# A two-layer hybrid attention trunk on one core: the causal mask of the stick-breaking mixer moved from identity matmuls to VectorE adds in PSUM, and the output stage split in the middle

## The chip, the core and the metric

The kernel runs on one core of a Trainium2 chip. The core has a matmul engine (TensorE, PE in the profile, with its weight loads as PEld), three elementwise engines (VectorE is DVE, ScalarE is ACT, GpSimd is POOL) and a queue engine (SyncE, SP) that here only issues transfers. Each engine runs its own list of instructions in order and waits on semaphores for the others. TensorE writes to PSUM, eight banks of 512 float32 per partition, and VectorE and ScalarE read and write there as well. The metric is the time of one execution on the device in microseconds, as the median of several runs.

## What is computed

Two layers on 512 tokens of width 1024. A layer normalises its input, projects it to some 8,000 columns, runs three causal token mixers (A: sparse attention with a top-k choice of keys; B: a sliding window of 128; C: stick-breaking attention), gates and projects each mixer's output, adds the three and projects the sum back onto the residual stream. A last RMS norm gives the output. Mixer C is the one whose mask is touched:

```python
strict = (key_pos[None, :] < qpos[:, None])[None, None]
z = jnp.einsum('bthd,bshd->bhts', qb, k).astype(jnp.float32) * (dh ** -0.5)
log_beta = jax.nn.log_sigmoid(z)
log_1m = jnp.where(strict, jax.nn.log_sigmoid(-z), 0.0)
after = lax.cumsum(log_1m, axis=3, reverse=True) - log_1m
a = jnp.where(strict, jnp.exp(log_beta + after), 0.0)
return jnp.einsum('bhts,bshd->bthd', a.astype(v.dtype), v)
```

and the output stage is `x + gate * (merged @ w_out)`, after the last layer followed by `y * rsqrt(mean(x*x) + EPS) * g`.

## The kernel before

Everything is kept with features or keys laid out so that TensorE works on 128x128 weights and up to 512 columns. Each float32 product is made of three matmuls in a faster 32-bit type: a matrix is split into a high part (a cast) and a remainder (a subtraction), and high x high, high x low and low x high are summed in PSUM. So for each weight tile that arrives (`wstage`), a cast makes `whi` and a subtraction makes `wlo`. Either may run on several engines.

The order of the work is not written by hand. The program is recorded as a list of instructions, some with alternatives on two or three engines, and a planner (`Recorder`) plays it forward with prices for each operation (`price`), picks at each step an engine and an instruction by priority, takes new priorities from the latest possible starts (`latest`), repeats this five times and keeps the best (`order`). The order it ends with is what each engine runs. GpSimd operations that share a memory port with VectorE get an explicit dependency on the VectorE operation ahead of them. All instructions are emitted from one line (L596 in the profile; pairs of small tiled matmuls from L594), so groups are told apart by their tiles.

A layer's stages: `first_phase` and `v_phase` project the first columns and the values. Then the three mixers run one after another, C first, woven with the projections of what comes later (`uh`, `ul` times `whi`, `wlo` into the banks `ps_z`), with the top-k search of mixer A (`score`, on VectorE) and with the branch projections. Last comes `out_phase`.

Mixer C takes its 8 heads in 4 pairs. For a pair, `c_qk` fills five banks `ps_s` with scores: nine matmuls of `KH` and `klow` against `Q`, and for each of 4 query blocks and 2 heads one matmul of an identity with a mask in bfloat16 (`ident_b`, `cmask_b`), which adds a large negative number on and above the diagonal of the last 128 columns. Seven small matmuls (`low_parts`) add the low parts of the keys; in pairs 1 to 3 the values of the pair before (`t`, `vc`) ride in the same instruction group and are then evacuated by `finish_pair` (`e`, `Y`). Then each bank goes through an absolute value (on ScalarE or VectorE), an exponential, a logarithm, a minimum with a subtraction, a reverse scan (VectorE) and a last exponential; the result `t` is transposed by TensorE (20 transposes with the identity in `small`) for the product with the values. The banks are released by the scans.

`out_phase` makes eight output tiles from the merged branches (`mh`, `ml`, which lie in the buffers `vc`, `va`, `Q`, `KH`). The last two (`tail`) are made in two column parts, so that the norm of the first part can start before the second is done. `update` adds the residual, squares, sums the squares into `m` and scales by the final gain; `rstd` sums over partitions by a matmul with `nones` and takes the logarithm and the exponential; `after` multiplies and, in the last layer, sends the products out. In layer 0 the parts are 256 and 256 columns, in the last layer 320 and 192.

`load_consts` loads the rotary tables and the masks and casts identity and mask to bfloat16.

Of the kernel before, what the change touches and what calls it, by code (L numbers as in the profile page):

```python
# [260 lines left out]
class Recorder:  # L261
# [75 lines left out]
    def price(self, x, engine, op, args, kw):  # L337
# [17 lines left out]
        if engine == "PE":  # L355
# [6 lines left out]
            elif op == "transpose":  # L362
                c, y.mode = 0.1085, "t"
                y.cost, y.lag = c, c + self.PIPE
            else:
                rhs, y.mode = args[2], "m"
                c = 4 * n / 2.4e3 + 0.01 if rhs.dtype == F32 else 0.06 if rhs.dtype == BF16 else (n + 33.5) / 2.4e3
                y.cost, y.lag = c, c + self.PIPE
# [41 lines left out]
    def forward(self):  # L410
# [38 lines left out]
        while len(out) < len(self.list):  # L449
# [51 lines left out]
            if y.mode == "dma":  # L501
                x.end = dma_free = max(at + (2.1 if at < 20.0 else 3.0), dma_free) + y.lag * (1.6 if dma_free < 5.5 else 0.955 if at < 20.0 else 1.0)
                lanes.append(x.end)
# [40 lines left out]
    def latest(self, end, out):  # L544

        late = {x.i: end - x.hold for x in out}
        after, first = {}, {}
# [76 lines left out]
def trunk(ctx, tc, xT, vecs, w_ss, w_gt, w_first, w_t, w_v, w_br, w_o, rope, consts, out):  # L624
# [541 lines left out]
    def c_qk(p):  # L1166
        def fn():
# [3 lines left out]
            for i in (3, 2, 0, 1):  # L1171
# [7 lines left out]
                for e in range(2):  # L1179
                    mm(o[e], q[:, e, ts], kh[:, e, :W], first[e])  # L1180
                for e in range(2):
                    mm(o[e][:, W - 128:], ident_b, cmask_b, False)
                if i == 1:
                    mm(o[1], q[:, 1, ts], kl[:, S:], False)
            low_parts(q, kl, apos, zb, "c", p, LOW_ALL)
            for bk in (0, 3, 1, 4, 2):
                z = zb[bk]
                t = pt[bk] = t512("t", 10)
                u32 = mybir.dt.uint32
# [273 lines left out]
    def out_phase(l):  # L1463
# [34 lines left out]
        def after(cs_):  # L1498
            rstd(cs_)
            if l + 1 < L:  # L1500
                if cs_.start == 0:
                    st["uh"], st["ul"] = [None] * KT, [None] * KT
                for k in (0, 1):
                    times_rstd(st["xn"][k], cs_)
                    make_u(l + 1, k, st["xn"][k], cs_)
                return
            w = cs_.stop - cs_.start
            for d in range(KT):
                if d % 2 == 0 or w > S // 2:
                    o, n = t512("t", 10), 0  # L1510
                v, a = o[:, n:n + w], st["xn"][d][:, cs_]
                n += w
                if d in (2, 4):
                    POOL.tensor_tensor(out=v, in0=a, in1=st["rstd_sb"][:, cs_], op=OP.mult)
                else:
                    DVE.tensor_tensor(out=v, in0=a, in1=st["rstd"][:, cs_], op=OP.mult)
                if w > S // 2:
                    SP.dma_start(out[:, d, cs_], v)
                elif d % 2:
                    SP.dma_start(out[:, d - 1:d + 1, cs_], o[:, :n].rearrange("p (a b) -> p a b", a=2))  # L1520

# [8 lines left out]
        def tail(*ws):  # L1530
            z, xr = [zbank(), zbank()], [load(6), load(7)]
            for cs_ in HALVES if l + 1 < L else (slice(0, 320), slice(320, S)):
                for i in range(2):
                    mms(6 + i, ws[2 * i:2 * i + 2], z[i], cs_)
                    update(6 + i, z[i], xr[i], cs_)
                after(cs_)
            save(6)
            save(7)
            st["x"] = st["xn"]
            if l + 1 < L:  # L1540
                st["xold"] = st["xsave"]
# [77 lines left out]

    sin_t = cos_t = tri0 = band = ident_b = cmask_b = None  # L1620

    def load_consts():
        nonlocal sin_t, cos_t, tri0, band, ident_b, cmask_b
        late = f(st["uh"][4][:, 0:1])
# [7 lines left out]
        tri0, band = cb[:, 0:512], cb[:, 512:768]  # L1632
        cc = t512("t", 10)[:, :128]
        POOL.tensor_copy(out=cc[:, 0:1], in_=late)
        SP.dma_start(cc, consts[:, 768:896])
        ident_b = fixed("ident_b", [P, P], BF16)
        POOL.tensor_copy(out=ident_b, in_=ident)
        cmask_b = fixed("cmask_b", [P, P], BF16)
        POOL.tensor_copy(out=cmask_b, in_=cc[:, :P])

# [91 lines left out]
```

## Time and profile before

| what | value |
|---|---|
| median of 3 runs | 1168.36 us (1167.31 to 1169.35) |
| the profiled execution: time | 1167.32 us |
| the profiled execution: span from first to last instruction | 1165.5 us |
| mean granted TensorE clock | 0.998 |
| instructions | 17679 |
| transferred in the span | 139.40 MB, a mean of 120 GB/s |

The profile is of one execution. Its page gives, for each engine, the time in which it was busy; the chain of work that ended last; groups of like instructions with their count, total and mean time, and what ended the idle time before them. A timeline row is: start in us from the first instruction, duration, engine, line, operation, output and inputs, shape, count; in brackets the idle time before it and what ended that. A row of the chain is start, duration, engine and output tile, with the number of instructions merged into it. A row of the windows gives the stretch, its length, the busy time and the count of PE, PEld, DVE, ACT and POOL, the granted clock, the busy share of the transfer engines and GB/s. A matmul's row shows its whole passage (0.39 us for 512 columns), while the next one starts earlier, so rates are read from starts. Layer 0's mixer C runs from about 121 to 217 us, layer 1's from 692 to 788, and the last layer's `tail` begins at 1143.9.

### The profile page before, as it was taken

Reading aid. Unit: us, or ns where it says so; the run is one execution under the profiler, and the core shown is the slowest. Engines: PE = TensorE matmul, PEld = TensorE weight load, DVE = VectorE, ACT = ScalarE, POOL = GpSimd, SP = SyncE. Lnnn points to the kernel's source line nnn. Section 1 sums busy time; section 2 is a strip of 40 time slices with the busy share of each in tenths; the row PEclk is TensorE's granted clock in tenths of the full one; section 3 lists DMA queues with packets and bytes.
Section 4 is the critical chain, followed back from the end, with each engine's and each line's share of the span. In section 5 each row is a group of like instructions: output and inputs, shape, how many; then the busy total and the mean of one; then the engine's idle time right before and its main releaser. Section 6 shows DMA issues by size and latency. Waiting matters only on the chain.

```text
span 1165.5 us, 17679 instructions
## 1 busy us (share of the span) xinstructions
PE 1155.3 (99%) x5963; PEld 965.2 (83%) x5963; DVE 969.8 (83%) x2219; ACT 546.7 (47%) x1153; POOL 147.2 (13%) x197
## 2 busy tenths in 40 slices
PE   9999999999999999999999999999999999999997
PEld 7899777888888887788889987778888888877886
DVE  7967999999898986878687599999998988566765
ACT  6623766652565642432134157664545665242222
POOL 0100343421000000000000015443100010000000
PEclk9999999999999999999999999999999999999999
DMA  9644322433334444345544433334333333223342
GB/s 355 228 116 124 98 73 82 118 117 109 110 112 123 128 138 143 100 129 179 167 121 110 125 99 84 80 91 126 108 99 109 94 92 98 100 83 91 99 129 98
DMA packets 80539, 139.40 MB, mean 120 GB/s; under 512 B 10048, under 2 KB 20544, under 8 KB 80448
## 3 DMA queue, kind: packets, MB, share of 16 engines
q1 hardware_dynamic: 79296, 136.17, 39.8%
q10 hardware_dynamic: 1152, 2.10, 0.5%
q8 instruction: 47, 0.77, 0.3%
q14 instruction: 44, 0.36, 0.1%
HBM read 125.39 MB, written 4.19 MB: 111 GB/s over the span
## 4 chain that ended last, share of the span: by engine, by line
PE 96%; DVE 2%; DMA 1%; issue 0%; SPq 0%; ACT 0%; DVEq 0%; ACTq 0%
PE ps_z L596 73%; PE ps_s L596 18%; PE ps_s L594 4%; PE ps_z L594 2%; DVE t L596 1%; DMA Y<-in_w_ss 1%; DVE Y L596 0%; SPq L596 0%; DVE e L596 0%; DVE ul L596 0%; ACT uh L596 0%; DVE xm L596 0%; DVE Q L596 0%; DVE wlo L596 0%; ACT t L596 0%
## 5 line engine op out<-in xcount | busy, mean ns | idle before, releaser
L596 PE MATMUL ps_z<-uh,whi 128*128 128x512 f32 (+1 forms) x905 | 355.1, 394 | 0.3 <-ACT uh L596 0.3
L596 PE MATMUL ps_z<-uh,wlo 128*128 128x512 f32 (+1 forms) x905 | 351.9, 390 | 0.0
L596 PE MATMUL ps_z<-ul,whi 128*128 128x512 f32 (+1 forms) x905 | 351.1, 389 | 0.0
L596 DVE TENSOR_TENSOR wlo<-wstage,whi 128x512 fp32r<-128x512 f32 (+2 forms) x300 | 196.0, 656 | 15.6 <-ACT whi L596 6.3
L596 PEld LDWEIGHTS ps_z<-uh,whi 128*128 128x128 f32 x905 | 169.8, 188 | 35.4 <-issue 1.7
L596 PEld LDWEIGHTS ps_z<-uh,wlo 128*128 128x128 f32 x905 | 169.8, 188 | 34.7 <-issue 0.7
L596 PEld LDWEIGHTS ps_z<-ul,whi 128*128 128x128 f32 x905 | 170.0, 188 | 33.3 <-DVE ul L596 0.6
L596 DVE CAST whi<-wstage 128x512 fp32r<-128x512 f32 (+2 forms) x213 | 87.2, 410 | 122.2 <-PE ps_z L596 102.2
L596 ACT CAST whi<-wstage 128x512 fp32r<-128x512 f32 (+2 forms) x126 | 75.1, 600 | 147.9 <-PE ps_z L596 129.9
L596 POOL TENSOR_TENSOR wlo<-wstage,whi 128x512 fp32r<-128x512 f32 (+1 forms) x72 | 92.3, 1284 | 379.3 <-ACT whi L596 138.9
L596 PE MATMUL ps_z<-Y,whi 128*128 128x512 f32 x384 | 119.1, 391 | 0.0
L596 ACT ACTIVATE e<-ps_z 128x512 f32<-128x512 f32 x68 | 40.3, 594 | 120.0 <-PE ps_z L596 119.8
L596 PEld LDWEIGHTS ps_z<-Y,whi 128*128 128x128 f32 x384 | 71.6, 188 | 14.6
L596 ACT ACTIVATE t<-t 128x512 f32<-128x512 f32 x120 | 69.4, 627 | 18.0 <-DVE t L596 16.6
L596 ACT ACTIVATE e<-e 128x512 f32<-128x512 f32 x96 | 59.7, 631 | 36.6 <-DVE e L596 36.1
L596 PE MATMUL ps_z<-Y,wlo 128*128 128x512 f32 x192 | 74.8, 389 | 0.0
L596 ACT ACTIVATE t<-t,nm 128x256 f32<-128x256 f32 (+3 forms) x128 | 65.0, 509 | 9.9 <-DVE nm L596 9.8
L596 PEld LDWEIGHTS ps_s<-small,t 128*128 128x128 f32 x432 | 50.3, 140 | 7.7 <-ACT t L596 0.4
L596 PE MATMUL ps_s<-small,t 128*128 128x128 f32 x432 | 56.3, 273 | 0.1
L596 DVE MAX8 m<-score 128x8 f32<-128x256 f32 (+2 forms) x96 | 53.1, 555 | 1.2
L596 DVE MATCH_REPLACE8 score<-m,score 128x256 f32<-128x256 f32 (+2 forms) x96 | 52.0, 542 | 0.0
L596 PE MATMUL ps_s<-KH,Q 128*128 128x256 f32 (+3 forms) x280 | 50.7, 308 | 0.0
(218 smaller groups left out, 1938.8 us busy)
## 6 DMA issues: line engine op xcount, KB each, us to landing
wstage<-in_w_t SPq DMA_DIRECT2D x212, 256.0 KB, 2.7
wstage<-in_w_v SPq DMA_DIRECT2D x48, 182.0 KB, 2.3
m<-zs SPq DMA_DIRECT2D x128, 64.0 KB, 2.0
wstage<-in_w_gt SPq DMA_DIRECT2D x32, 256.0 KB, 2.7
wstage<-in_w_ss SPq DMA_DIRECT2D x32, 256.0 KB, 2.7
wstage<-in_w_o SPq DMA_DIRECT2D x32, 256.0 KB, 2.7
Y<-in_w_ss SPq DMA_DIRECT2D x15, 512.0 KB, 5.7
wstage<-in_w_first SPq DMA_DIRECT2D x16, 256.0 KB, 3.8
```

Source lines behind the costliest of these rows:

```text
L594: self.real[engine].matmul(*[real(a) for a in q[:3]], start=q[3], stop=True, skip_group_check=True)
L596: made = getattr(self.real[engine], y.op)(*[real(a) for a in y.args], **{k: real(v) for k, v in y.kw.items()})
```

## The change

The mask in mixer C is no longer a matmul. Five VectorE additions, one per bank, add the float32 mask in place in PSUM ahead of each bank's absolute value: on 128 columns for the two banks that hold one 512-wide block, on two groups of 128 for the three banks that hold two blocks. The bfloat16 identity and mask go, with their two casts. The last layer's `tail` is split 256 and 256, the products of the first part (`last`) are recorded behind the second part's updates and write to `Y` buffers, three of the eight on GpSimd, and all output transfers carry two tiles. Three of the planner's rules change: a matmul costs at least 0.112 us, a transfer out of the chip's buffers ends a fixed 2.1 us after its start and holds no other up, and the latest start of an instruction takes its full duration into account.

```diff
-                c = 4 * n / 2.4e3 + 0.01 if rhs.dtype == F32 else 0.06 if rhs.dtype == BF16 else (n + 33.5) / 2.4e3
+                c = 4 * n / 2.4e3 + 0.01 if rhs.dtype == F32 else 0.06 if rhs.dtype == BF16 else max(0.112, (n + 33.5) / 2.4e3)
...
-                x.end = dma_free = max(at + (2.1 if at < 20.0 else 3.0), dma_free) + y.lag * (1.6 if dma_free < 5.5 else 0.955 if at < 20.0 else 1.0)
+                if not x.writes:
+                    x.end = at + 2.1
+                else:
+                    x.end = dma_free = max(at + (2.1 if at < 20.0 else 3.0), dma_free) + y.lag * (1.6 if dma_free < 5.5 else 0.955 if at < 20.0 else 1.0)
...
-        late = {x.i: end - x.hold for x in out}
+        late = {x.i: end - max(x.hold, x.end - x.start) for x in out}
...
                 for e in range(2):
                     mm(o[e], q[:, e, ts], kh[:, e, :W], first[e])
-                for e in range(2):
-                    mm(o[e][:, W - 128:], ident_b, cmask_b, False)
                 if i == 1:
                     mm(o[1], q[:, 1, ts], kl[:, S:], False)
             low_parts(q, kl, apos, zb, "c", p, LOW_ALL)
             for bk in (0, 3, 1, 4, 2):
                 z = zb[bk]
+                if bk % 3:
+                    m = z[:, 256:].rearrange("p (a b) -> p a b", a=2) if bk != 2 else z.rearrange("p (a b) -> p a b", a=2)[:, :, 128:]
+                    DVE.tensor_tensor(out=m, in0=m, in1=cmask.unsqueeze(1).to_broadcast([P, 2, P]), op=OP.add)
+                else:
+                    DVE.tensor_tensor(out=z[:, 384:], in0=z[:, 384:], in1=cmask, op=OP.add)
                 t = pt[bk] = t512("t", 10)
...
+        def last(cs_):
             w = cs_.stop - cs_.start
             for d in range(KT):
-                if d % 2 == 0 or w > S // 2:
-                    o, n = t512("t", 10), 0
-                v, a = o[:, n:n + w], st["xn"][d][:, cs_]
-                n += w
-                if d in (2, 4):
+                if d % 2 == 0:
+                    o = rec.tile("Y", [P, 2 * S], F32) if cs_.start == 0 else t512("t", 10)
+                v, a = o[:, w * (d % 2):w * (d % 2) + w], st["xn"][d][:, cs_]
+                if d in ((1, 3, 5) if cs_.start == 0 else (2, 4)):
                     POOL.tensor_tensor(out=v, in0=a, in1=st["rstd_sb"][:, cs_], op=OP.mult)
                 else:
                     DVE.tensor_tensor(out=v, in0=a, in1=st["rstd"][:, cs_], op=OP.mult)
-                if w > S // 2:
-                    SP.dma_start(out[:, d, cs_], v)
-                elif d % 2:
-                    SP.dma_start(out[:, d - 1:d + 1, cs_], o[:, :n].rearrange("p (a b) -> p a b", a=2))
+                if d % 2:
+                    SP.dma_start(out[:, d - 1:d + 1, cs_], o[:, :2 * w].rearrange("p (a b) -> p a b", a=2))
...
-            for cs_ in HALVES if l + 1 < L else (slice(0, 320), slice(320, S)):
+            parts = HALVES if l + 1 < L else (slice(0, 256), slice(256, S))
+            for cs_ in parts:
                 for i in range(2):
                     mms(6 + i, ws[2 * i:2 * i + 2], z[i], cs_)
                     update(6 + i, z[i], xr[i], cs_)
+                if cs_.start and l + 1 == L:
+                    last(parts[0])
                 after(cs_)
+            if l + 1 == L:
+                last(parts[1])
...
-        cc = t512("t", 10)[:, :128]
-        POOL.tensor_copy(out=cc[:, 0:1], in_=late)
-        SP.dma_start(cc, consts[:, 768:896])
-        ident_b = fixed("ident_b", [P, P], BF16)
-        POOL.tensor_copy(out=ident_b, in_=ident)
-        cmask_b = fixed("cmask_b", [P, P], BF16)
-        POOL.tensor_copy(out=cmask_b, in_=cc[:, :P])
+        cmask = fixed("cmask", [P, P], F32)
+        POOL.tensor_copy(out=cmask[:, 0:1], in_=late)
+        SP.dma_start(cmask, consts[:, 768:896])
```

The planner's order changes with it at many places. Three of them follow, with a row per instruction: line, operation, output and inputs, shape, and a count where like instructions follow each other.

On TensorE, the transposes of mixer C's second pair in layer 0, behind the 48 projection matmuls that follow the pair's values (`small,t` is a transpose of `t` with the identity), before:

```order
L596 MATMUL ps_z<-uh_584,wlo 128x512
L596 MATMUL ps_s<-small,t 128x128 x13
L596 MATMUL ps_z<-uh_221,whi 128x512
L596 MATMUL ps_z<-ul_234,whi 128x512
L596 MATMUL ps_z<-uh_221,wlo 128x512
L596 MATMUL ps_s<-small,t 128x128 x3
L596 MATMUL ps_z<-uh_297,whi 128x512
L596 MATMUL ps_z<-ul_313,whi 128x512
L596 MATMUL ps_s<-small,t 128x128 x4
```

and in the changed kernel:

```order
L599 MATMUL ps_z<-uh_581,wlo 128x512
L599 MATMUL ps_s<-small,t 128x128 x10
L599 MATMUL ps_z<-uh_219,whi 128x512
L599 MATMUL ps_s<-small,t 128x128 x3
L599 MATMUL ps_z<-ul_232,whi 128x512
L599 MATMUL ps_z<-uh_219,wlo 128x512
L599 MATMUL ps_z<-uh_295,whi 128x512
L599 MATMUL ps_z<-ul_311,whi 128x512
L599 MATMUL ps_z<-uh_295,wlo 128x512
L599 MATMUL ps_s<-small,t 128x128 x3
```

Thirteen transposes stood together, three came 3 matmuls later and four 2 behind those. Now ten stand there, three one matmul on, three another 5 on, and the last four 15 matmuls behind the last row shown.

On VectorE, the same pair, from the evacuation of the values of the pair before (`e`, `Y`) to the first subtractions (`SCALAR_TENSOR_TENSOR t` on 512) and scans (on 511), before:

```order
L596 TENSOR_TENSOR e<-ps_z,G 128x512
L596 TENSOR_SCALAR t<-ps_s 128x512 x2
L596 TENSOR_TENSOR Y<-e,Y 128x512
L596 TENSOR_SCALAR t<-ps_s 128x512
L596 SCALAR_TENSOR_TENSOR t<-ps_s,t 128x512 x2
L596 MEMSET t 128x1
L596 SCALAR_TENSOR_TENSOR t<-ps_s,t 128x511 x2
```

and in the changed kernel:

```order
L599 TENSOR_TENSOR e<-ps_z,G 128x512
L599 TENSOR_TENSOR ps_s<-ps_s,cmask 128x128
L599 CAST Y<-e 128x512
L599 TENSOR_TENSOR ps_s<-ps_s,cmask 128x128
L599 TENSOR_TENSOR Y<-e,Y 128x512
L599 TENSOR_TENSOR ps_s<-ps_s,cmask 128x256 x2
L599 TENSOR_SCALAR t<-ps_s 128x512 x2
L599 SCALAR_TENSOR_TENSOR t<-ps_s,t 128x512 x2
L599 SCALAR_TENSOR_TENSOR t<-ps_s,t 128x511 x2
```

Four mask additions stand between the evacuation and the absolute values, the fifth comes later; one absolute value went to another engine and the cast of `Y` came.

On VectorE, the end of the program, from the sum of the first part's squares to the first product of the second part, before:

```order
L596 TENSOR_TENSOR m_11836<-m_11836,e 128x192
L596 TENSOR_TENSOR t<-xm_11829,ps_s 128x320
L596 TENSOR_TENSOR t<-xm_11873,ps_s 128x320
L596 TENSOR_TENSOR t<-xm_11963,ps_s 128x320
L596 TENSOR_TENSOR t<-xm_12048,ps_s 128x320
L596 TENSOR_TENSOR t<-xm_12082,ps_s 128x320
L596 TENSOR_TENSOR t<-xm_12113,ps_s 128x320
L596 SCALAR_TENSOR_TENSOR xm_12113<-ps_z,mods_77,G 128x192
L596 TENSOR_TENSOR e<-xm_12113 128x192
L596 TENSOR_SCALAR xm_12113<-xm_12113,small 128x192
L596 TENSOR_TENSOR t<-xm_11829,ps_s 128x192
```

and in the changed kernel:

```order
L599 TENSOR_TENSOR Y<-xm_11801,ps_s 128x256
L599 SCALAR_TENSOR_TENSOR xm_12054<-ps_z,mods_77,G 128x256
L599 TENSOR_TENSOR Y<-xm_11890,ps_s 128x256
L599 TENSOR_TENSOR Y<-xm_11978,ps_s 128x256
L599 TENSOR_TENSOR Y<-xm_12054,ps_s 128x256
L599 TENSOR_TENSOR Y<-xm_12084,ps_s 128x256
L599 TENSOR_TENSOR m_11808<-m_11808,e 128x256
L599 SCALAR_TENSOR_TENSOR xm_12084<-ps_z,mods_77,G 128x256
L599 TENSOR_SCALAR xm_12084<-xm_12084,small 128x256
L599 TENSOR_TENSOR t<-xm_11801,ps_s 128x256
```

Five products of the first part stand ahead of the last update, where six of 320 columns stood, the update of the seventh tile lies among them, and the last square is no longer VectorE's.

More of the change, by code (lines that the diff above doesn't have):

```diff
@@ L1618, in start @@
         ada_load(2)
-    sin_t = cos_t = tri0 = band = ident_b = cmask_b = None
+    sin_t = cos_t = tri0 = band = cmask = None
     def load_consts():
-        nonlocal sin_t, cos_t, tri0, band, ident_b, cmask_b
+        nonlocal sin_t, cos_t, tri0, band, cmask
         late = f(st["uh"][4][:, 0:1])
```

## The prediction

> **What bounds the kernel now.** I read the busy table first, then the chain of work that ended last, then the waits of TensorE, then the windows around the stick-breaking stage (mixer C).
>
> ```profile
> PE 1155.3 (99%) x5963; PEld 965.2 (83%) x5963; DVE 969.8 (83%) x2219; ACT 546.7 (47%) x1153; POOL 147.2 (13%) x197
> ...
> PE 96%; DVE 2%; DMA 1%; issue 0%; SPq 0%; ACT 0%; DVEq 0%; ACTq 0%
> ...
> PE ps_s L596 <- DVE t L596: 2.3, 3, 1.0
> ...
> 121.00:217.00 96.00, 95.90 (x528) 75.10 (x526) 93.00 (x174) 67.66 (x121) 42.84 (x65) 1.00 0.32 85
> 692.00:788.00 96.00, 96.00 (x530) 75.33 (x528) 93.29 (x176) 67.37 (x121) 43.07 (x66) 1.00 0.32 86
> ```
>
> TensorE (PE) is busy for 1155.3 of 1165.5 us and makes up 96% of the chain. Its longest class of wait is 2.3 us in all. The last two rows are the four head pairs of mixer C in layer 0 and in layer 1 (columns: length, then PE, weight load, VectorE, ScalarE, GpSimd busy): PE never pauses there, and VectorE (DVE) is busy for 93.0 and 93.3 of 96 us. So a matmul taken away shortens the program, unless VectorE, with 3.0 and 2.7 us to spare in those stages, can't carry what it gets instead.
>
> **The change part by part: masks off TensorE.** Per head pair 8 identity matmuls go, 64 in all. What they cost on the path is read from two rows of the chain: the score matmuls of a C pair (9 score matmuls and 8 masks) and of a pair of mixer A, which issues the same 9 without masks.
>
> ```profile
> 140.45 2.06 PE ps_s L596 x17
> 143.28 2.30 PE ps_z L594 x16
> 145.59 11.12 PE ps_z L596 x48
> ...
> 368.02 1.38 PE ps_s L596 x9
> 370.19 2.30 PE ps_z L594 x16
> ```
>
> The blocks last 2.06 and 1.38 us, and the next listed block follows 0.77 and 0.79 us after each, so the 8 masks cost 0.68 us per pair. Eight pairs (4 per layer) give **8 x 0.68 = 5.4 us off the path**. The other bound is the start of a mask pair to the start of the matmuls behind it:
>
> ```profile
> 140.75 0.29 PE L596 MATMUL ps_s<-cmask_b,ident_b 128*128 128x128 bf16 x2
> 140.84 0.60 PE L596 MATMUL ps_s<-KH,Q 128*128 128x384 f32 x2
> ```
>
> 0.09 us for two, 32 such twos: 2.9 us. The rest of the 0.68 then would be the change between the two types, which goes with the masks too, so I take 5.4 and keep 2.9 as an end.
>
> **Masks onto VectorE.** Five adds per pair come: two on 128 columns and three on 256, in place in PSUM. No row shows such an add, but mixer B's mask add, from PSUM to SBUF, has both widths:
>
> ```profile
> L596 DVE CUSTOM_DVE_ANT_0 t<-ps_s,cb 128x256 f32<-128x256 f32 x48 | 17.3, 420 | 0.1
> L596 DVE CUSTOM_DVE_ANT_0 t<-ps_s,cb 128x128 f32<-128x128 f32 x32 | 8.1, 286 | 0.0
> ```
>
> 2 x 0.286 + 3 x 0.420 = 1.83 us per pair, 7.3 us per layer, more than the 3.0 us that VectorE has to spare there. An add in place in PSUM may be cheaper, and then VectorE only gains time; or as dear as the update of 256 columns further down, 0.48 us, with 0.13 less for 128 columns as between the two rows here: 2 x 0.35 + 3 x 0.48 = 2.14 us per pair, 8.6 per layer. I take 1.83, from the nearest operation. The planner takes other work off VectorE. Counted in both orders from the first pair's low key parts to the last pair's evacuation, each layer loses on VectorE 3 weight casts, 3 weight remainders, 2 absolute values, 2 clamps, one key cast, one Q remainder and one top-k step, and gains 3 casts of Y, one scaled Q and one rotary product:
>
> ```profile
> L596 DVE CAST whi<-wstage 128x512 fp32r<-128x512 f32 x171 | 72.6, 425 | 94.6 <-PE ps_z L596 85.2 <-PE ps_s L596 6.5 <-issue 1.6
> L596 DVE TENSOR_TENSOR wlo<-wstage,whi 128x512 fp32r<-128x512 f32 x238 | 163.2, 686 | 13.5 <-ACT whi L596 6.0
> L596 DVE TENSOR_SCALAR t<-ps_s 128x512 uint32<-128x512 uint32 x22 | 14.4, 684 | 0.1
> ```
>
> Off: 3 x 0.425 + 3 x 0.686 + 2 x 0.684 = 4.7, and about 3.1 for the rest at like widths; on: 3 x 0.425 + 0.69 + 0.69 = 2.7. Net load per layer: 7.3 + 2.7 - 7.8 = +2.2 us against 3.0 and 2.7 spare. It fits, barely, so I cost the adds at nothing. (By the dear end it is +3.5, and 2 x 3.5 - 5.7 = 1.3 us come back.) Their cover is TensorE's stream of projections, 48 matmuls between a pair's values and its transposes. If the cover is gone, PE stands before the transposes. There is no slack at that place today:
>
> ```profile
> 155.69 0.63 ACT L596 ACTIVATE t<-t 128x512 f32<-128x512 f32 x1 [0.40 <-DVE t L596]
> ...
> 156.54 1.58 PE L596 MATMUL ps_s<-small,t 128*128 128x128 f32 x13
> ```
>
> An exponential ends at 156.32 and the 13 transposes start at 156.54. But the new order moves them. In pair 1, 10 of the 13 stay behind 48 matmuls and 3 go one matmul later; the next 3 go from 51 to 54, and the 4 of the bank that is masked last from 53 to 69, 16 matmuls later (3.7 us, by the 11.12 us of 48 above). That answers a chain that is longer by 1.83 us. What stands behind a mask on VectorE is the pair's own absolute values, and in pairs 1 to 3 the masks themselves stand behind the gate product that waits for the values of the pair before, as the absolute values did.
>
> **The Trainium skill, against it.** The work that leaves VectorE goes partly to GpSimd. The Trainium skill, "SBUF — State Buffer", section "Who interferes with whom", says that a VectorE cast, or an operation with two SBUF inputs, and a GpSimd operation that reads SBUF block each other for a whole instruction. The sum by this page would be that of the second rival below, which is worked out from rows; the page also says that an operation with one SBUF input doesn't contend, and the new adds are of that kind.
>
> **Constants.** Two casts on GpSimd and a staging tile go in the first phase, on an engine that is busy 13% of the time: nothing.
>
> **The output stage.** The last two output tiles are split 256/256 in place of 320/192. Rates of the matmuls, by starts:
>
> ```profile
> 1143.92 0.30 PE L596 MATMUL ps_z<-vc,whi 128*128 128x320 f32 x1
> ...
> 1150.96 0.25 PE L596 MATMUL ps_z<-vc,whi 128*128 128x192 f32 x1
> ...
> 1156.72 0.27 PE L596 MATMUL ps_z<-va,wlo 128*128 128x192 f32 x1
> ...
> 581.76 4.67 PE ps_z L596 x39
> ```
>
> 48 matmuls of 320 take 7.04 us (0.147 each). The 48 of 192 take 5.87, with one sum for the norm (0.54) among them, so 0.111 each: not 0.6 of 0.147. Layer 0 already splits 256/256: 4.67 / 39 = 0.120. New: 96 x 0.120 + 0.50 = 12.0 against 12.9 us, and the stream ends at 1155.94, not 1156.83. All of this is in the clock of the old trace, without the 5.4 us. Behind the stream:
>
> ```profile
> 1155.47 2.47 DVE L596 TENSOR_TENSOR t<-xm,ps_s 128x320 f32<-128x320 f32 x6
> 1157.86 0.41 DVE L596 SCALAR_TENSOR_TENSOR xm<-ps_z,mods,G 128x192 f32<-128x192 f32 x1
> ...
> 1160.17 1.68 DVE L596 TENSOR_TENSOR t<-xm,ps_s 128x192 f32<-128x192 f32 x6 [1.15 <-ACT ps_s L596]
> ```
>
> Today six products of the first part hold VectorE until 1157.9, so the last update starts 1.03 us after the stream. In the new order five products (0.33 us each), one update and one sum stand ahead of it. The first part's stream ends at 1143.92 + 48 x 0.120 = 1149.7, its sum for the norm goes 15 matmuls later, at 1151.5, and its products begin 0.74 + 0.47 + 0.41 us (below) behind that, at 1153.1; 5 x 0.33 + 0.48 + 0.42 = 2.6 us of work is done by 1155.7, before the update can start. The new tail is then a copy of layer 0's:
>
> ```profile
> 579.29 0.28 PE L596 MATMUL ps_z<-vc,whi 128*128 128x256 f32 x1
> 579.49 0.48 DVE L596 SCALAR_TENSOR_TENSOR xm<-ps_z,mods,G 128x256 f32<-128x256 f32 x1 [1.42 <-PE ps_z L596]
> 580.07 0.42 ACT L596 ACTIVATE e<-xm 128x256 f32<-128x256 f32 x1 [2.46 <-DVE xm L596]
> ...
> 587.97 0.70 PE L596 MATMUL ps_s<-m,nones 128*128 128x256 f32 x2
> 588.71 0.45 ACT L596 ACTIVATE ps_s<-ps_s,epst 128x256 f32<-128x256 f32 x1 [1.25 <-PE ps_s L596]
> 589.18 0.37 ACT L596 ACTIVATE ps_s<-ps_s 128x256 f32<-128x256 f32 x1
> 589.59 0.75 DVE L596 TENSOR_TENSOR xm<-xm,ps_s 128x256 f32<-128x256 f32 x2 [1.67 <-ACT ps_s L596]
> ```
>
> From the end of the stream: 0.20 to the update, 0.58 to the square, 0.46 to the sum, 0.74 to the logarithm, 0.47 to the exponential, 0.41 to the products: 1158.80. Six products, 5 x 0.33 + 0.42 = 2.07, end at 1160.87, against 1160.17 + 1.68 = 1161.85: 0.98 earlier. But the last part is a third larger:
>
> ```profile
> 1162.00:1164.00 2.00, 0.00 (x0) 0.00 (x0) 0.00 (x0) 0.00 (x0) 0.00 (x0) 0.50 1.03 348
> 1164.00:1165.50 1.50, 0.00 (x0) 0.00 (x0) 0.00 (x0) 0.00 (x0) 0.00 (x0) 0.50 0.00 0
> ```
>
> The last figure of the first row is 348 GB/s. Its 0.786 MB take 2.26 us at that rate, 1.049 MB take 3.01. If the transfers bind from the first issue (two products done at 1159.55, not 1160.73) the end moves by -1.18 + 0.75 = -0.43; if the last issue binds, -0.98 + 0.19 = -0.79. I take the middle, **-0.6 us**.
>
> **Sum.** -5.4 - 0.6 = -6.0 us. The profiled execution took 1167.32 us (span 1165.5 and 1.8 around it), so it becomes 1161.3; the median of the runs, 1168.36, lies 1.0 above that execution, and with the same difference becomes **1162.3**.
>
> **Rivals.**
> *First: the masks delay the transposes and PE waits there.* For it: VectorE's 97% in the stage and the 0.2 us of slack above. Against: the transposes moved by up to 3.7 us. With half of the 1.83 us returned in each pair, 8 x 0.91 = 7.3 us come back: 1169.6, no measurable change. It decides from 0.46 us per pair.
> *Second, slower: VectorE becomes the bound because GpSimd's additional work blocks it.* In the C stages 3 remainders and 3 casts per layer move, on GpSimd 1.28 and 0.61 us each (first rows below): 2 x 3 x 1.89 = 11.4 us of blocking, with a net load of 2 x 2.2 and 5.7 us of spare time: 10.1 us come back, 1172.4. It is slower than before by over 0.2% from 8.4 us on. Against it:
>
> ```profile
> L596 POOL TENSOR_TENSOR wlo<-wstage,whi 128x512 fp32r<-128x512 f32 (+1 forms) x72 | 92.3, 1284 | 379.3 <-ACT whi L596 138.9
> L596 POOL CAST whi<-wstage 128x512 fp32r<-128x512 f32 x31 | 19.0, 612 | 66.3 <-DVE klow L596 37.5 <-PE ps_z L596 17.2 <-DVE score L596 4.8
> 157.21 1.28 POOL L596 TENSOR_TENSOR wlo<-wstage,whi 128x512 fp32r<-128x512 f32 x1 [0.69 <-ACT whi L596]
> ...
> 156.69 1.20 DVE L596 TENSOR_TENSOR_SCAN t<-ps_s,t 128x511 f32<-128x511 f32 x1
> 157.92 0.69 DVE L596 TENSOR_TENSOR klow<-ps_z,KH 64x512 fp32r<-64x512 f32 x1
> ```
>
> A remainder on GpSimd runs beside a scan and a subtraction that read PSUM, and neither gets longer: such work is laid beside PSUM operations, of which there are now more.
> *Third: the change doesn't do what it says.* The PE time freed is lost again to weights that are split too late, now that ScalarE and GpSimd split more of them, and only the tail gains: 1168.36 - 0.6 = 1167.8, the same. For it: a cast and a remainder take 0.61 + 1.28 us on GpSimd and 0.43 + 0.69 on VectorE. Against: PE's waits for weights are too short to be among its classes of wait today.
>
> **How the numbers follow.** About 0.2% (2.3 us) is what a measurement here can tell from no change. Forecast 0.83, rival 1 0.09, rival 3 0.04, rival 2 0.04: faster 0.83, same 0.13, slower 0.04. Low end: the profiled execution's own 1167.32 - 5.4 - 0.8, less 1 us as the runs spread: 1160.0. High end: masks worth 2.9 and the tail 0.43 give 1165.0; with 0.8 us of waits in the C stages (the dear end gives 1.3) 1165.8. Rivals 1 to 3 stay outside and hold 0.17.
>
> **What would show it.** Right: no gap in PE in the C stages, score blocks of 1.4 us, VectorE near 95 of 96 us there, and in the tail the last products 6.4 us earlier in the span (5.4 + 1.0) and its end 5.8 to 6.2 us earlier. Wrong: a wait of PE for the exponentials ahead of transposes (rival 1), longer VectorE rows beside GpSimd's (rival 2), or PE waiting for `whi`/`wlo` (rival 3). A mask add far above 0.42 us would break the load sum.

## The result, and the profile after

The changed kernel takes 1161.76 us, the median of 5 runs (1161.1 to 1162.65), against 1167.61 (1167.31 to 1169.35) for the kernel before on the same chip: a ratio of 0.9946, 95% interval 0.9932 to 0.9961. That is 5.85 us less, and 0.5 us below the forecast. The profiled execution has a span of 1160.0 us at a granted clock of 0.998.

The busy table, the chain's shares by engine, the longest waits of TensorE, and the windows of mixer C in both layers (pairs 1 to 4, moved with the earlier start of layer 1):

```profile
PE 1149.7 (99%) x5899; PEld 962.1 (83%) x5899; DVE 965.5 (83%) x2220; ACT 551.0 (47%) x1167; POOL 167.8 (14%) x220
...
PE 97%; DVE 1%; DMA 1%; ACT 0%; SPq 0%; issue 0%; DVEq 0%
...
PE ps_s L599 <- DVE t L599: 1.3, 2, 0.8
...
121.00:217.00 96.00, 96.00 (x515) 76.36 (x514) 94.55 (x187) 67.50 (x124) 53.44 (x74) 1.00 0.33 90
689.00:785.00 96.00, 96.00 (x516) 76.38 (x515) 94.49 (x186) 67.26 (x124) 53.40 (x74) 1.00 0.32 90
```

TensorE still has no pause in the two C stages. VectorE is busy for 94.5 of 96 us there, GpSimd for 53.4 where it had 43, and the matmuls are the 64 fewer.

The chain in pair 2 of layer 0, from its scores to its last transposes:

```profile
140.19 1.38 PE ps_s L599 x9
...
142.36 2.30 PE ps_z L597 x16
144.66 11.12 PE ps_z L599 x48
155.78 1.09 PE ps_s L599 x10
...
157.11 0.33 PE ps_s L599 x3
157.44 1.17 PE ps_z L599 x5
158.61 0.36 PE ps_s L599 x3
158.97 3.44 PE ps_z L599 x15
162.41 0.44 PE ps_s L599 x4
```

The score block lasts 1.38 us with its 9 matmuls. The 48 projections start at 144.66 and end at 155.78, where the first ten transposes start: no gap. The other ten lie where the new order put them.

The groups of mask additions, and VectorE's remainders (total busy time, mean ns):

```profile
L599 DVE TENSOR_TENSOR ps_s<-ps_s,cmask 128x256 f32<-128x256 f32 x24 | 9.4, 421 | 0.0
L599 DVE TENSOR_TENSOR ps_s<-ps_s,cmask 128x128 f32<-128x128 f32 x16 | 4.5, 292 | 0.1
L599 DVE TENSOR_TENSOR wlo<-wstage,whi 128x512 fp32r<-128x512 f32 x231 | 158.5, 687 | 14.0 <-ACT whi L599 6.5
```

How much a C stage got shorter is read between two marks on TensorE: the first scores of C and the first scores of A behind it. Timeline rows of the changed kernel, both layers:

```profile
121.74 1.13 PE L599 MATMUL ps_s<-KH,Q 128*128 128x512 f32 x6
...
339.51 1.42 PE L599 MATMUL ps_s<-KH,Q 128*128 128x512 f32 x8
...
689.62 1.42 PE L599 MATMUL ps_s<-KH,Q 128*128 128x512 f32 x8
...
907.43 1.42 PE L599 MATMUL ps_s<-KH,Q 128*128 128x512 f32 x8
```

The same marks in the kernel before:

```profile
121.03 0.61 PE L596 MATMUL ps_s<-KH,Q 128*128 128x512 f32 x2
...
341.50 1.42 PE L596 MATMUL ps_s<-KH,Q 128*128 128x512 f32 x8
...
691.75 0.61 PE L596 MATMUL ps_s<-KH,Q 128*128 128x512 f32 x2
...
911.96 1.42 PE L596 MATMUL ps_s<-KH,Q 128*128 128x512 f32 x8
```

The stretches are 217.77 and 217.81 us, and were 220.47 and 220.21: 2.70 and 2.40 us went, **5.10 us** in all.

The end of the program, the first and the last matmul of the tail, then VectorE, ScalarE, TensorE and the transfers behind it, and the GB/s in the last stretches:

```profile
1139.42 0.28 PE L599 MATMUL ps_z<-vc,whi 128*128 128x256 f32 x1
...
1151.25 0.28 PE L599 MATMUL ps_z<-va,wlo 128*128 128x256 f32 x1
...
1151.57 0.48 DVE L599 SCALAR_TENSOR_TENSOR xm<-ps_z,mods,G 128x256 f32<-128x256 f32 x1
...
1154.22 2.08 DVE L599 TENSOR_TENSOR t<-xm,ps_s 128x256 f32<-128x256 f32 x6 [1.33 <-ACT ps_s L599]
...
1155.00 2.08 SPq L599 DMA_DIRECT2D out<-t  x4
...
1156.00:1157.00 1.00, 0.00 (x0) 0.00 (x0) 0.29 (x1) 0.00 (x0) 0.12 (x1) 0.50 1.08 379
1157.00:1158.00 1.00, 0.00 (x0) 0.00 (x0) 0.00 (x0) 0.00 (x0) 0.00 (x0) 0.50 1.08 381
1158.00:1159.00 1.00, 0.00 (x0) 0.00 (x0) 0.00 (x0) 0.00 (x0) 0.00 (x0) 0.50 0.74 258
```

From the first to the last matmul of the tail it is 11.83 us (12.80 before), to the end of the last product 16.88 (17.93), to the end of the span 20.58 (21.58): **1.0 us**. Spans are printed to 0.1 us, so a time that ends with the span is good to 0.05 us. The last update now starts 0.32 us after the last matmul's start instead of 1.14.

The two stretches and the tail give 6.1 us, the spans differ by 5.5. The rest lies ahead of mixer C: its first scores came at 121.74 instead of 121.03, which the repeat below takes apart. What lies between the A scores and the next mark changed by 0.14 us and less.

### The profile page after: what moved, and what is told of

It is laid out like the page before. It is cut to its first block, busy times and chain, and to the rows that moved or that the text cites. A ratio compares the mean times of both kernels' runs of the same rounds, so it can differ in the third digit from the quotient of the medians.

```text
span 1160.0 us, 17615 instructions
## 1 busy us (share of the span) xinstructions
PE 1149.7 (99%) x5899; PEld 962.1 (83%) x5899; DVE 965.5 (83%) x2220; ACT 551.0 (47%) x1167; POOL 167.8 (14%) x220
## 4 chain that ended last, share of the span: by engine, by line
PE 97%; DVE 1%; DMA 1%; ACT 0%; SPq 0%; issue 0%; DVEq 0%
PE ps_z L599 74%; PE ps_s L599 18%; PE ps_s L597 4%; PE ps_z L597 2%; DMA Y<-in_w_ss 1%; DVE Y L599 0%; SPq L599 0%; DVE t L599 0%; ACT uh L599 0%; DVE ul L599 0%; ACT amul L599 0%; DVE wlo L599 0%; DVE xm L599 0%; ACT zs L599 0%; ACT whi L599 0%
## 5 line engine op out<-in xcount | busy, mean ns | idle before, releaser
L599 DVE TENSOR_TENSOR wlo<-wstage,whi 128x512 fp32r<-128x512 f32 (+2 forms) x293 | 191.4, 656 | 16.2 <-ACT whi L599 6.8
L599 DVE CAST whi<-wstage 128x512 fp32r<-128x512 f32 (+2 forms) x200 | 81.9, 410 | 121.4 <-PE ps_z L599 100.8
L599 POOL TENSOR_TENSOR wlo<-wstage,whi 128x512 fp32r<-128x512 f32 (+1 forms) x79 | 101.3, 1286 | 354.9 <-ACT whi L599 137.9
L599 ACT CAST whi<-wstage 128x512 fp32r<-128x512 f32 (+2 forms) x131 | 78.3, 601 | 131.5 <-PE ps_z L599 106.5
L599 PE MATMUL ps_s<-whi,ul 128*128 128x364 f32 x144 | 47.5, 330 | 0.0
```

The lines of the kernel that those rows point to most:

```text
L599: made = getattr(self.real[engine], y.op)(*[real(a) for a in y.args], **{k: real(v) for k, v in y.kw.items()})
```

## The experiments

Times are medians, of 5 to 11 runs. Each ratio is to runs of the kernel before on the same chip at the same time; these had 1167.61 us (changed), 1167.87 (after_again, mask_alone, tail_alone, no_adds), 1168.07 (adds_twice, rules_alone, order_320, split_276 and, again, split_alone, split_288) and 1168.14 (the narrow and wide additions). "Stretch" is the one from C to A above, first layer 0, then layer 1. The tail's three numbers run from its first matmul to its last, to the end of the last product, and to the end of the span.

| kernel | us | ratio to before (95%) | stretches | tail |
|---|---|---|---|---|
| before | 1167.61 | 1 | 220.47, 220.21 | 12.80, 17.93, 21.58 |
| changed | 1161.76 | 0.9946 (0.9932 to 0.9961) | 217.77, 217.81 | 11.83, 16.88, 20.58 |
| after_again | 1161.37 | 0.9943 (0.9931 to 0.9956) | 217.79, 217.83 | 11.82, 16.87, 20.58 |
| mask_alone | 1163.13 | 0.9958 (0.9945 to 0.997) | 217.85, 217.86 | 12.80, 17.93, 21.63 |
| tail_alone | 1166.86 | 0.999 (0.9981 to 0.9999) | 220.17, 220.26 | 11.83, 16.88, 20.61 |
| no_adds | 1161.93 | 0.9948 (0.9936 to 0.996) | 217.82, 217.66 | 11.83, 16.87, 20.52 |
| adds_twice | 1169.30 | 1.0011 (1.0002 to 1.002) | 221.54, 221.32 | 11.83, 16.88, 20.52 |
| adds_narrow_twice | 1162.21 | 0.9947 (0.9935 to 0.996) | 217.80, 217.90 | 11.83, 16.87, 20.59 |
| adds_wide_twice | 1164.53 | 0.9969 (0.9958 to 0.998) | 218.94, 219.05 | 11.82, 16.86, 20.60 |
| rules_alone | 1167.55 | 0.9995 (0.9986 to 1.0003) | 220.20, 220.26 | 12.90, 17.51, 21.17 |
| split_alone | 1167.05 | 0.9991 (0.9982 to 1.0) | 220.50, 220.21 | 11.83, 17.15, 20.83 |
| order_320 | 1162.00 | 0.9949 (0.9936 to 0.9961) | 217.72, 217.84 | 12.91, 17.39, 20.74 |
| split_276 | 1162.73 | 0.9953 (0.9939 to 0.9966) | 217.72, 218.10 | 11.82, 16.97, 21.39 |
| split_288 | 1162.46 | 0.9948 (0.9935 to 0.9962) | 217.78, 218.17 | 12.16, 17.08, 20.79 |

### The two parts apart, and a repeat

**mask_alone** is the changed kernel with the output stage and the three planner's rules of before. **tail_alone** is the kernel before with that output stage and those rules, and its masks on TensorE. **after_again** has no edit.

```diff
 mask_alone, against the changed kernel
-            parts = HALVES if l + 1 < L else (slice(0, 256), slice(256, S))
-            for cs_ in parts:
+            for cs_ in HALVES if l + 1 < L else (slice(0, 320), slice(320, S)):
...
 tail_alone, against the changed kernel
+                for e in range(2):
+                    mm(o[e][:, W - 128:], ident_b, cmask_b, False)
...
-                    DVE.tensor_tensor(out=m, in0=m, in1=cmask.unsqueeze(1).to_broadcast([P, 2, P]), op=OP.add)
...
-                    DVE.tensor_tensor(out=z[:, 384:], in0=z[:, 384:], in1=cmask, op=OP.add)
```

> The kernel before with the mask part alone: 64 identity matmuls out, 40 VectorE adds in, the old output stage and the old planner rules. Theory (the matmuls leave TensorE's path at 0.68 us per head pair and the adds are covered): 5.0 to 5.8 us less than before, C score blocks of 1.38 us, no wait of TensorE in the C stages over 1 us in all. Rival (the adds return part of it through waits ahead of the transposes): 3 to 4.6 us less, with the missing time between the first C scores and the first A scores of a layer. Second rival (an identity matmul costs only its spacing of 0.045 us): about 2.9 us less.

> The changed kernel with the masks back on TensorE: only the output stage and the planner's three rules differ from before. Theory: 0.6 to 1.1 us less than before, all of it behind the start of the last two output tiles, whose matmuls take 12.0 us in place of 12.9. Rival (the larger last transfers eat the gain): within 0.3 us of before. Rival (the planner's rules change the rest of the order too): a difference outside of the last 23 us of the span.

> The changed kernel once more, for a second trace. Theory (the 0.7 us by which its first C scores came later than before is the arrival of the first weights and differs from run to run): the first C scores start at another time than 121.90 us, anywhere from 121.0 to 122.5, and the intervals behind it repeat within 0.1 us. Rival (the change costs 0.7 us in the first phase): again 121.8 to 122.0.

The masks alone bring 4.74 us (1167.87 to 1163.13), a little under the 5.0 to 5.8 that were expected; its two stretches lost 4.97. The output stage with the rules brings 1.01. The sum, 5.75, is about what both bring together, 5.85 and 6.50. In the traces the parts are clean: mask_alone has the short stretches and the old tail, tail_alone the reverse.

In the repeat C's first scores stand at 121.80, in the range that was given to the rival, and in part the rival is right. From the first projection to the first scores of C both traces of the changed kernel take 105.88 us, the kernel before 105.55: 0.33 of the 0.71 us repeat, so they go with the changed kernel and not with the single execution. Neither part alone has them (105.64 in mask_alone, 105.60 in tail_alone); the fourteen traces take 105.5 to 106.4. The other 0.38 us is the first projection itself, which starts at 15.86 and 15.92 in the changed kernel, at 15.48 before, and between 15.5 and 17.0 in the fourteen traces. Whether the kernel or the single execution sets it is open: the two traces of the changed kernel agree there, but two earlier blocks of TensorE (`t`, `nones`) start at 7.31 and 8.92 us in the one and at 7.90 and 9.91 in the other. Kernels are compared by the stretches for that reason.

### What the additions cost

**no_adds** leaves mixer C's causal mask out altogether.

```diff
-                if bk % 3:
...
-                    DVE.tensor_tensor(out=m, in0=m, in1=cmask.unsqueeze(1).to_broadcast([P, 2, P]), op=OP.add)
-                else:
-                    DVE.tensor_tensor(out=z[:, 384:], in0=z[:, 384:], in1=cmask, op=OP.add)
```

> The changed kernel without any causal mask in mixer C: neither the matmuls nor the adds. Theory (the adds are covered by TensorE's projections): within 0.6 us of the changed kernel, 5.6 to 6.6 us less than before. Rival (the adds cost time on the path, as the difference of 0.9 us between 8 x 0.68 and what the profiles show ahead of the output stage suggests): 0.8 us or more below the changed kernel.

Without any addition the stretches are 217.82 and 217.66: 0.1 us less in both layers together. The additions are hidden in full: the order that the planner makes around them costs no time. The windows of no_adds hold a surprise:

```profile
121.00:217.00 96.00, 95.90 (x510) 76.14 (x510) 94.02 (x178) 68.58 (x123) 45.27 (x68) 1.00 0.31 89
689.00:785.00 96.00, 96.00 (x513) 76.47 (x512) 94.02 (x180) 68.57 (x124) 45.90 (x68) 1.00 0.31 90
```

VectorE is busy for 94.0 us there, only 0.5 less than with 7.3 us of additions, and GpSimd for 8 us less: the planner fills VectorE either way. So its busy share doesn't say how much it could still take. Three kernels with more additions measured that.

```diff
 adds_twice (the mask has half the value)
-                    DVE.tensor_tensor(out=m, in0=m, in1=cmask.unsqueeze(1).to_broadcast([P, 2, P]), op=OP.add)
+                    for _ in range(2):
+                        DVE.tensor_tensor(out=m, in0=m, in1=cmask.unsqueeze(1).to_broadcast([P, 2, P]), op=OP.add)
...
-                    DVE.tensor_tensor(out=z[:, 384:], in0=z[:, 384:], in1=cmask, op=OP.add)
+                    for _ in range(2):
+                        DVE.tensor_tensor(out=z[:, 384:], in0=z[:, 384:], in1=cmask, op=OP.add)
...
 adds_wide_twice (adds_narrow_twice has the same line for z[:, 384:] in its place)
+                    DVE.tensor_tensor(out=m, in0=m, in1=zmask.unsqueeze(1).to_broadcast([P, 2, P]), op=OP.add)
```

> The changed kernel with each mask addition made twice with half the value (same sum): 10 additions per pair instead of 5, and an order planned anew. Theory (the additions are free only because VectorE had room: 94.5 of 96 us are used in a C stage, so 1.5 us are left): 7.3 us more per layer do not fit, and what the planner cannot move to ScalarE and GpSimd stops TensorE: 2 to 12 us more than the changed kernel's 1161.6, the stretch from the first scores of C to the first scores of A longer than 217.8 us, VectorE at 95.5 or more of 96. Rival (VectorE's load is of no account in this stage, since work is moved off it at no cost): within 0.8 us of the changed kernel, the stretch still 217.8.

> The changed kernel with a second addition, of zeros, behind each mask addition on 128 columns: 2 x 0.292 us more per pair, 2.3 us per layer. With all five doubled (7.3 us per layer) half came back: the stretch from the first scores of C to the first scores of A grew by 3.6 us a layer. Theory A (a fixed spare time of 1.5 us, the 96 - 94.5 us of the window): the stretch grows by 0.8 us per layer, the time by about 1.6. Theory B (a threshold: the planner can move some 3.7 us per layer to other engines, and only what is beyond it comes back): the stretch stays at 217.8 us, the time within 0.5 us of the changed kernel. Theory C (no threshold, half of any addition comes back): 1.2 us per layer.

> The changed kernel with a second addition, of zeros, behind each mask addition on two groups of 128 columns: 3 x 0.421 us more per pair, 5.05 us per layer. Theory A (1.5 us of spare time): the stretch from C to A grows by 3.5 us per layer, the time by about 7. Theory B (a threshold near 3.7 us per layer): by 1.4 us per layer, the time by about 2.8. Theory C (half of any addition): by 2.5 us per layer, the time by about 5.

With 2.3, 5.05 and 7.3 us more of additions per layer the stretch grows by 0.06, 1.2 and 3.6 us (means of both layers): nothing at first, then all that lies beyond some 3.7 us (7.3 - 3.6 = 3.7, 5.05 - 1.2 = 3.85). That is the course of Theory B, a threshold. It was formed from adds_twice, so the other two tested it; the fixed 1.5 us of Theory A and the half of Theory C both fail at the narrow additions. The 0.06 us is no difference: split_276 and split_288, whose edit is in the tail, have stretches 0.3 and 0.36 us longer in layer 1. For adds_twice the theory foretold the loss, but not VectorE's share, which was to reach 95.5. Its windows, and its transposes in layer 0's stage by groups (busy, mean, idle before them):

```profile
121.00:217.00 96.00, 94.22 (x486) 74.17 (x485) 94.00 (x193) 66.29 (x121) 49.28 (x74) 1.00 0.30 86
689.00:785.00 96.00, 94.54 (x485) 74.53 (x485) 94.39 (x198) 64.82 (x119) 48.71 (x73) 1.00 0.29 89
...
L599 PE MATMUL ps_s<-small,t 128*128 128x128 f32 x76 | 12.9, 275 | 1.3 <-DVE t L599 1.2
```

TensorE stops ahead of the transposes, as the first rival had it, with VectorE at 94.0 and 94.4, no busier than without any mask. The chain of work that ended last then runs through VectorE. Four pieces of it in pairs 2 and 3 (start, duration):

```profile
174.66 0.49 DVE score L599 x2
175.18 1.23 DVE ps_s L599 x5
...
178.93 4.01 DVE t L599 x5
...
189.93 0.50 PE ps_s L599
```

A step of mixer A's top-k search, additions, the work behind them, then the next scores of TensorE. The transposes need no top-k step, so it is the queue of VectorE that holds TensorE up, and not only a longer way of one bank to its transposes.

Where room for more additions came from shows when the C stage is cut at its own end: from its first scores to the last matmul of its last pair's values (`t`, `vc`), layer 0, in no_adds, changed, adds_wide_twice and adds_twice:

```profile
122.63:215.84 93.21, 93.11 (x495) 73.87 (x494) 91.28 (x172) 67.48 (x121) 44.75 (x67) 1.00 0.30 86
...
121.74:215.78 94.04, 94.04 (x502) 74.72 (x501) 92.60 (x182) 67.25 (x123) 53.44 (x74) 1.00 0.32 88
...
122.01:220.05 98.04, 97.65 (x516) 76.49 (x515) 96.29 (x191) 73.06 (x132) 49.22 (x73) 1.00 0.32 91
...
122.21:224.88 102.67, 100.89 (x525) 79.03 (x524) 100.60 (x207) 68.99 (x126) 53.90 (x79) 1.00 0.31 90
```

The first 7.3 us raise VectorE's busy time by 1.3 us only, and GpSimd's by 8.7: the rest of the load was moved. Of the 5.05 and 7.3 us on top a quarter and nothing leave: VectorE is busy 3.7 and 8.0 us longer than in the changed kernel, and the stage is 4.0 and 8.6 us longer. TensorE is kept busy with projections that stood behind the stage before: 299 and 309 matmuls with `whi` or `wlo` lie in it instead of 288, at 0.23 us each (48 take 11.12 us) 2.5 and 4.9 us. That leaves 1.5 and 3.7 us, close to the growth of the stretches, 1.2 and 3.8 in this layer.

### The output stage

```diff
 rules_alone: the kernel before with the three changed rules of the planner
 split_alone: the kernel before with
-            for cs_ in HALVES if l + 1 < L else (slice(0, 320), slice(320, S)):
+            for cs_ in HALVES:
 order_320, split_276, split_288: the changed kernel with 320, 276 and 288 in place of 256, as in
-            parts = HALVES if l + 1 < L else (slice(0, 256), slice(256, S))
+            parts = HALVES if l + 1 < L else (slice(0, 320), slice(320, S))
```

> The kernel before with only the three changed rules of the planner: masks on TensorE, output stage 320 and 192 in the old code. Theory (the rules bring nothing by themselves): within 0.5 us of the kernel before, stretches from C to A 220.2 to 220.5 us, last product 17.9 us after the tail's first matmul. Rival (the rules are part of the gain): 0.6 us or more below the kernel before.

> The changed kernel with the old split, 320 and 192, but the new order of the first part's products and the new transfers. Theory (of the 1.05 us by which the last product came earlier, the order is worth about 0.8 and the split 0.25): stream 12.8 to 12.9 us as before, last product 17.1 to 17.3 us after the tail's first matmul, time 0 to 0.4 us above the changed kernel. Rival (the split makes it, 0.9 us of stream): last product 17.6 or later, time 0.6 to 1.0 above.

> The kernel before with the last two output tiles split 256 and 256 and nothing else: masks on TensorE, old rules, old code for the products and transfers. Theory (the split by itself clears the way: the first part's six products are done 0.7 us before the second part's last update is due, and the new code adds nothing): stream 11.9 us, last product 16.9 us after the tail's first matmul, span end 20.6 us after it, time 0.7 to 1.2 us below the kernel before. Rival (the order of the products in the new code is needed, as the changed kernel with the old split had 0.84 of the 1.0 us): last product 17.4 us or more, time within 0.5 us of the kernel before.

> The changed kernel with the last two output tiles split 276 and 236 instead of 256 and 256. Theory (a matmul costs (columns + 33.5) / 2400 us above a floor of 0.111, so the stream stays 11.95 us; behind it only the width of the second part counts): last product 0.1 to 0.3 us earlier than the changed kernel's 16.88 us after the tail's first matmul, the time 0.1 to 0.4 us lower. Rival (the first part's wider products hold VectorE when the second part's update is due, as in the kernel before): last product 0.2 to 0.6 us later.

> The changed kernel with the last two tiles split 288 and 224. With 276 and 236 the last product came at 16.97 us and the end of the span 4.4 us behind it instead of 3.7. Theory (rows of 944 bytes are slow to write, rows that are a multiple of 128 bytes are not): end of the span 3.4 to 3.7 us after the last product, last product 16.9 to 17.2, time within 0.4 us of the changed kernel. Rival (any uneven pair of parts written two tiles at a time is slow): 4.2 us or more, time 0.6 to 1.1 us above.

What the three rules do by themselves was missed: nothing in the C stages, as expected, but the last product comes 0.42 us earlier. The time, 0.52 us below before, is no difference that was measured (the interval holds 1). The row ahead of the last update on VectorE differs; rules_alone:

```profile
1155.50 2.47 DVE L599 TENSOR_TENSOR t<-xm,ps_s 128x320 f32<-128x320 f32 x6
1157.88 0.36 DVE L599 TENSOR_TENSOR m<-m,e 128x192 f32<-128x192 f32 x1
1158.15 0.42 DVE L599 SCALAR_TENSOR_TENSOR xm<-ps_z,mods,G 128x192 f32<-128x192 f32 x1
```

The six products start right after the seventh tile's update, whose square went to ScalarE, and the last update comes 0.62 us after the last matmul's start (1157.53). In split_alone the split alone does it:

```profile
1153.20 2.08 DVE L596 TENSOR_TENSOR t<-xm,ps_s 128x256 f32<-128x256 f32 x6 [1.78 <-ACT ps_s L596]
1155.20 0.48 DVE L596 SCALAR_TENSOR_TENSOR xm<-ps_z,mods,G 128x256 f32<-128x256 f32 x1
...
1156.50 0.48 DVE L596 SCALAR_TENSOR_TENSOR xm<-ps_z,mods,G 128x256 f32<-128x256 f32 x1
```

The products are over at 1155.28, before the last matmul starts (1155.90). The end of the span, counted from the tail's start, comes some 0.75 us earlier with the split alone, 0.84 with the new order and the old split (order_320), and 1.0 with both: each clears VectorE ahead of the last update, and they don't add up. In both traces the last product lies between theory and rival: 17.39 us, between 17.3 and 17.6 (order_320), and 17.15, between 16.9 and 17.4 (split_alone). The times side with the theories, 0.24 us above the changed kernel and 1.02 us below the kernel before; the interval of the second ends at 1.

The narrower last parts brought nothing. With 276 and 236 the last product comes 0.09 us later, not earlier, and the end 0.8 later. The transfers, by issue (count, KB each, median us from issue to landing), of split_276, split_288 and the changed kernel:

```profile
out<-t SPq DMA_DIRECT2D x4, 236.0 KB, 3.1
```

```profile
out<-t SPq DMA_DIRECT2D x4, 224.0 KB, 2.3
```

```profile
out<-t SPq DMA_DIRECT2D x4, 256.0 KB, 2.3
```

With 288 and 224 the span ends 3.71 us after the last product, as in the changed kernel (3.70); with 276 and 236 it was 4.42. That fits slow rows of 944 bytes against rows of 896 and 1024. The first part's transfers fit as well: 276 KB in rows of 1104 bytes took 3.4 us to land, 320 KB in rows of 1280 (order_320) 2.7. Which property of a row decides wasn't tried. The time of split_288 is 0.7 us above the changed kernel, more than the 0.4 that its theory allowed; 0.36 of it is the longer stretch in layer 1. No version beats the changed kernel: the medians of these three lie 0.2 to 1.4 us above its two, and their intervals overlap with its own.

## Why the prediction was right

**Masks off TensorE: right, 5.4 forecast, 5.1 measured.** The score blocks are 1.38 us, as forecast. The C stages lost 5.10 us, and even without any additions no more than 5.2, so the stretches lost 0.64 us per pair, not 0.68. That is too near for a cause: a new order alone moves a stretch by up to 0.36 us. The other end, 2.9 us, is out, because the change between the types went with the masks. In the kernel before the two score matmuls of 384 columns behind a pair of masks start at 140.84 (shown in the prediction) and the next masks follow 0.44 us later:

```profile
141.28 0.29 PE L596 MATMUL ps_s<-cmask_b,ident_b 128*128 128x128 bf16 x2
```

In the changed kernel the same two take 0.35 us. Added up from start to start over layer 0's stretch, the 32 masks take 1.52 us and the score matmuls between and behind them 0.95 us more than in the changed kernel, together 0.62 us per pair.

**Additions hidden: right, but by more room than was worked out, and not for the reason given.** Their durations were 421 and 292 ns for 420 and 286 forecast, and VectorE's 94.5 us are the "near 95". The net load on VectorE, +2.2 us forecast, is +1.5 (93.0 to 94.5). But the 3.0 us "to spare" were no measure: some 3.7 us more per layer still fit behind the 7.3. "It fits, barely" is the statement that falls, and VectorE's busy share would have looked the same in a kernel that loses time (94.0 in adds_twice). Theory B gave the amounts, but its mechanism, work moved to other engines until no more can move, is not what the windows of the stage show: in adds_wide_twice and adds_twice most or all of the added load stays on VectorE, the C stage gets longer, and TensorE fills it with later projections. What sets how many of these can be drawn forward was not tried.

**Rival 1 (masks delay the transposes)** didn't come here, but its mechanism is real: adds_twice shows it, at twice the additions. **Rival 2 (blocking by GpSimd)** falls: GpSimd got 10 us more work per stage, and VectorE's remainders stayed at 687 ns (686 before); no row here shows the blocking that the Trainium skill, "SBUF — State Buffer", section "Who interferes with whom", describes; whether the explicit dependencies of the kernel keep such pairs apart wasn't tried. **Rival 3 (only the tail gains)** falls with mask_alone.

**Output stage: right in its mechanism, too small, -0.6 forecast, -1.0 measured.** Stream and chain came as worked out: last product 1.05 us earlier, forecast 0.98. The step that was mis-sized is the last transfers, taken to give 0.19 to 0.75 us back at 348 GB/s. They ran at some 380, and the end follows the last product by 3.70 us, before by 3.65: nothing was given back. Larger last transfers still cost something. The last four of the kernel before, by issue, landed in 2.1 us, the new ones in 2.3:

```profile
out<-t SPq DMA_DIRECT2D x4, 192.0 KB, 2.1
```

And order_320, with 192 columns last but 8 output transfers instead of 12, ends 3.35 us after its last product. The kernel before, mask_alone and rules_alone, with 12, end 3.65 to 3.70 us after theirs. What costs them the 0.3 us isn't settled.

**Sum.** -6.0 forecast, -5.85 measured. The two sizes, 0.3 too much and 0.4 too little, cancel: that the sum came so close is luck, while the path of each part was foreseen. The forecast of 1162.3 started from a median of 1168.36; in the later runs the kernel before stands at 1167.6 to 1168.1. Two signs did not come: the last products are 5.55 us earlier in the span (1161.85 to 1156.30) and its end 5.5, where 6.4 and 5.8 to 6.2 were named. The later start of mixer C, 0.71 us, had no term in the prediction.

## What to carry to other kernels

Where a planner spreads work over engines, an engine's busy share is its choice and no measure of room: double the suspected load, and look for the amount from which the bounding engine's own stretch grows. Look at the length of the loaded stage as well: it can grow unseen while work drawn forward from later stages fills it. Read a gain between two marks on the bounding engine, since the first projection alone stood up to 1.5 us apart in these traces. And where two edits remove the same wait, each tried alone shows nearly the whole gain.

## What was not expected of the hardware

Additions in place in PSUM cost what the nearest operation from PSUM to SBUF cost: 292 and 421 ns against 286 and 420. The tail's matmuls of 276 and 236 columns took as long as those of 256 (11.82 against 11.83 us), of 288 and 224 0.33 more and of 320 and 192 1.0 to 1.1 more: matmuls of 192, 224 and 236 columns all start 0.111 to 0.112 us apart. And 4 transfers of 236 KB took 3.1 us to land where 4 of 256 KB took 2.3.
